# An encoder trunk's final norm begun one expert sooner, its low parts taken off GpSimd, and chunk 0 multiplied ahead of chunk 1

## The chip, the cores and the metric

The kernel runs on one core of a Trainium2 chip. The metric is device time in microseconds (us). An execution's own time holds the span of the profile, from the first to the last instruction, and about 2 us around it.

## The reference, cut to what matters

A two-layer encoder over 1024 tokens of 1024 values, in float32. Each layer is a mixer and then 16 experts; each expert takes the 128 tokens that want it most, and the results are added onto the stream. A last norm follows.

```python
def rmsnorm(x, g):
    y = x * rsqrt(mean(x * x, axis=-1) + EPS)
    return y * g

def ec_moe(h, w_router, w_gate, w_up, w_down):      # 16 experts, 128 tokens each
    aff = softmax(h @ w_router)
    gates, idx = top_k(aff.T, 128)                  # expert e: its tokens idx[e]
    xs = h[idx]
    y = silu(xs @ w_gate) * (xs @ w_up) @ w_down
    return zeros.at[idx].add(y * gates)

for i in range(2):
    x = x + mixer[i](rmsnorm(x, norm_mix[i]))       # starts with one projection h @ w_in
    x = x + ec_moe(rmsnorm(x, norm_ffn[i]), ...)
return rmsnorm(x, final_norm)
```

## The kernel before

The 1024 tokens are eight chunks of 128 rows, one row per partition. Products keep float32's accuracy by splitting each operand into a high part (`hi`, rounded by ACT's copy) and a low part (`lo = x - hi`, L232, L236, L149): `mm3` (L258) issues three matmuls for one. Weights come as pieces of 128 x 1024 values (512 KB) through the class `Stream`: `load` (L185) issues a piece's DMA on SP's queue into a free slot, `conv` (L212) makes its `hi` on ACT (L225) and its `lo` on DVE, or on POOL where `pool` is set, and gives the slot back.

**Experts** (`out_moe`, L285, called for each layer). One expert has twelve pieces: four each for the up, gate and down products. PE's order is written out by hand (L717 to 764): up of expert e with the transposes of expert e+1's rows in it (`xsT`, L581), then gate of e+1 with the transposes of e's hidden rows `sg` in it (`hT`, L624, L628), then down of e. `prod` (L620) makes `sg` on DVE after up. `index(e + 3)` (L568) makes a later expert's row numbers by eight small matmuls and gathers its rows by an indirect DMA on POOL (L578); `onehot` (L562) feeds it on DVE. `scatter` (L651) scales the result on ACT (`y`, L655) and adds it to the stream `xres` in DRAM by an indirect DMA on POOL (L659). After the products of piece j, `ahead(j)` (L593) converts up to piece j+7 into one of eight `hi`/`lo` pairs; every twelfth low part goes to POOL (`EVERY`), 15 per layer. In layer 1 the ring of slots holds 27 pieces (7 + 15 + 5). ACT, DVE and POOL each run their work in the order in which it is issued here.

**Final norm** (layer 1 alone). `final_load` (L668), after the scatter of expert 14, loads all eight chunks of `xres` on SP and gathers the rows of expert 15 as a ninth block. `final` (L694), after expert 15's down products, takes sums of squares on ACT (L690), reciprocal roots in steps (`rsqrt_steps`, L121; those of the eight chunks on POOL, with two pairs of chunks ahead of the gain row, which PE and ACT spread over the partitions, L702, L703), multiplies on DVE (`mult`, L681) and writes each chunk on SP (L685). Rows of expert 15 get its result added (L712) and are normed last and written over the chunks' rows by an indirect DMA (L715).

**Starts.** `even_proj` (L834) and `odd_proj` (L1409) begin their layer with `NormProj`: `load` a chunk, `trans` (L782) transposes it on PE and splits it (L148, L149), `stat` (L795) makes its reciprocal root on DVE, `mm` (L798) multiplies it with eight row blocks `kk` of the weights. The PSUM tiles `pt` of the transposes come from a pool of two (layer 0) or four (layer 1).

## Time and profile before

| | us |
|---|---|
| median of 3 runs (2040.78 to 2044.11) | 2043.83 |
| profiled execution, its own time | 2040.48 |
| its span | 2038.7 |
| PE busy | 1867.7 (92%) |
| DVE busy | 1507.7 (74%) |
| ACT busy | 1245.2 (61%) |
| POOL busy | 504.1 (25%) |

The experts of layer 0 lie at about 645 to 961 us, those of layer 1 at about 1690 to 2004, the final norm behind them to the end; layer 0 starts at 0, layer 1 at about 970. Shares are means over stages with different limits, so each stage is read by itself. A time in a row is in us from the span's start.

### The profile page before, as it was taken

To read this page: it belongs to the slowest core of one execution; us is meant where nothing else is said; L and a number is where in the kernel's file an instruction comes from. 1 tells how busy PE (TensorE), PEld (TensorE's weight loads), DVE (VectorE), ACT (ScalarE), POOL (GpSimd) and SP (SyncE) were. 2 spreads that over 40 slices of the span, in tenths; PEclk is the share of its full clock that TensorE was granted. 3 is DMA by queue.
4 is the path that set the end of the run, shared out by engine and by line. 5 is a ranking of instruction groups with operands and counts; after the bars stand their busy time and mean duration, and the time that the engine had idled before them with its cause. 6 is when DMAs were issued, how large, how long until landed. Compare 5 with 4: busy or idle time off the path is not lost. (4 is left out here: it accounts for less than half of the span.)

```text
span 2038.7 us, 29998 instructions
## 1 busy us (share of the span) xinstructions
PE 1867.7 (92%) x10350; PEld 1563.4 (77%) x10350; DVE 1507.7 (74%) x3092; ACT 1245.2 (61%) x2020; POOL 504.1 (25%) x426
## 2 busy tenths in 40 slices
PE   8999999998995999998998799999998968999993
PEld 6888899997883777776887688888886846777772
DVE  5431246776557999997776688889995569999994
ACT  5322257775324777776634688889883326877783
POOL 0010100002102443541002243322212014444334
PEclk9999999999997999999899999999999979999996
DMA  6232355542555999994326554424115848999955
GB/s 228 71 104 78 128 138 136 128 122 85 207 208 181 378 384 373 373 385 95 124 78 209 95 75 87 69 45 54 37 30 163 305 169 311 384 372 387 375 183 196
DMA packets 214171, 384.78 MB, mean 189 GB/s; under 512 B 71937, under 2 KB 122881, under 8 KB 214018
## 3 DMA queue, kind: packets, MB, share of 16 engines
q1 hardware_dynamic: 190082, 303.43, 45.6%
q0 software_dynamic: 21200, 73.13, 12.0%
q10 hardware_dynamic: 2736, 6.29, 0.9%
q8 instruction: 82, 1.34, 0.3%
q14 instruction: 71, 0.58, 0.1%
HBM read 309.13 MB, written 66.32 MB: 184 GB/s over the span
## 5 line engine op out<-in xcount | busy, mean ns | idle before, releaser
L232 DVE TENSOR_TENSOR lo<-raw,hi 128x1024 fp32r<-128x1024 f32 x243 | 334.0, 1416 | 12.2 <-ACT hi L225 12.2
L225 ACT ACTIVATE hi<-raw 128x1024 fp32r<-128x1024 f32 x269 | 275.1, 1055 | 15.3 <-PE py L644 12.1
L259 PE MATMUL pp<-hi,hT 128*128 128x512 f32 (+2 forms) x576 | 213.2, 370 | 0.0
L260 PE MATMUL pp<-lo,hT 128*128 128x512 f32 (+2 forms) x576 | 211.6, 367 | 0.1
L261 PE MATMUL pp<-hi,hT 128*128 128x512 f32 (+2 forms) x576 | 211.2, 367 | 0.0
L1866 DVE TENSOR_REDUCE nm<-css 128x1 f32<-128x1024 f32 x128 | 156.0, 1219 | 41.3 <-PE css L1860 40.8
L149 DVE TENSOR_TENSOR PT<-cpt,PT 128x512 fp32r<-128x512 f32 x256 | 163.1, 678 | 4.3 <-ACT PT L148 1.9
L148 ACT ACTIVATE PT<-cpt 128x512 fp32r<-128x512 f32 x256 | 139.6, 597 | 40.4 <-PE cpt L1884 38.7
L1860 PE MATMUL css<-kT,qT 128*128 128x512 f32 x512 | 151.7, 398 | 10.8 <-ACT pe L1872 9.5
L1872 ACT ACTIVATE pe<-css,nm 128x1024 f32<-128x1024 f32 x128 | 143.8, 1123 | 11.6 <-DVE rinv L1892 7.7
L1884 PE MATMUL cpt<-csident,pe 128*128 128x128 f32 x1024 | 135.0, 274 | 1.1 <-DVE PT L149 0.8
L1884 PEld LDWEIGHTS cpt<-csident,pe 128*128 128x128 f32 x1024 | 116.8, 141 | 16.3 <-DVE PT L149 3.7
L261 PEld LDWEIGHTS pp<-hi,hT 128*128 128x128 f32 x576 | 109.4, 190 | 17.5
L260 PEld LDWEIGHTS pp<-lo,hT 128*128 128x128 f32 x576 | 109.5, 190 | 17.3 <-DVE lo L236 0.3
L259 PEld LDWEIGHTS pp<-hi,hT 128*128 128x128 f32 x576 | 109.7, 190 | 17.1
L1860 PEld LDWEIGHTS css<-kT,qT 128*128 128x128 f32 x512 | 96.0, 189 | 34.6 <-ACT pe L1872 10.9
L1902 PE MATMUL po<-PT,vv 128*128 128x512 f32 x256 | 112.4, 439 | 7.1 <-DVE o L1910 7.1
L1179 DVE CUSTOM_DVE_ANT_0 sm<-ass,csnat 128x256 f32<-128x256 f32 x176 | 67.4, 420 | 52.3 <-PE ass L1177 47.6
L1903 PE MATMUL po<-PT,vv 128*128 128x512 f32 x256 | 101.6, 397 | 0.0
L232 DVE TENSOR_TENSOR cT<-raw,cT 128x1024 fp32r<-128x1024 f32 x65 | 95.7, 1492 | 3.3 <-ACT cT L225 3.2
L578 POOL DMA_INDIRECT xs<-hd,idx x32 | 65.9, 2060 | 128.3 <-DVE gt L576 128.3
L1177 PE MATMUL ass<-kT,qT 128*128 128x256 f32 x384 | 96.4, 381 | 1.0 <-DMA kT<-kT 1.0
(447 smaller groups left out, 4819.5 us busy)
## 6 DMA issues: line engine op xcount, KB each, us to landing
raw<-in_moe_w_up_dram SPq DMA_DIRECT2D x112, 512.0 KB, 6.2
raw<-in_moe_w_down_dram SPq DMA_DIRECT2D x110, 512.0 KB, 6.2
raw<-in_moe_w_gate_dram SPq DMA_DIRECT2D x106, 512.0 KB, 6.5
attn<-in_moe_w_gate_dram SPq DMA_DIRECT2D x22, 512.0 KB, 6.5
attn<-in_moe_w_down_dram SPq DMA_DIRECT2D x18, 512.0 KB, 5.9
raw<-in_even_w_in_dram SPq DMA_DIRECT2D x16, 512.0 KB, 4.7
hd<-h POOLq DMA_DIRECT2D x16, 512.0 KB, 5.5
attn<-in_moe_w_up_dram SPq DMA_DIRECT2D x16, 512.0 KB, 6.5
```

The source lines that it names most:

```text
L148: self.nc.scalar.activation(hi, src, AF.Copy)
L149: (eng or self.nc.vector).tensor_tensor(lo, src, hi.bitcast(F32), op=ALU.subtract)
L225: nc.scalar.activation(hv, tv, AF.Copy)
L232: (nc.gpsimd if pool else nc.vector).tensor_tensor(lv, tv, hv.bitcast(F32), op=ALU.subtract)
L259: nc.tensor.matmul(out, ah, bh, start=first, stop=False)
L260: nc.tensor.matmul(out, ah, bl, start=False, stop=False)
L261: nc.tensor.matmul(out, al, bh, start=False, stop=last)
L1860: nc.tensor.matmul(ss[:, n], a[:, sl], m[:, n * 512:(n + 1) * 512], start=(j == 0), stop=(j == len(passes) - 1))
L1866: nc.vector.tensor_reduce(nm, B[b]["ss"], axis=AX.X, op=ALU.max, negate=True)
L1872: nc.scalar.activation(pe, B[b]["ss"], AF.Exp, bias=B[b]["nm"], accum_out=l)
L1884: nc.tensor.transpose(pt[:, kk], B[b]["pe"][:, kc * 128:(kc + 1) * 128], k.ident)
L1902: nc.tensor.matmul(po[g], vv[:, kc], PT[g][:, 0, kc], start=(kc == 0), stop=False)
```

## The change

1. Low parts: `ahead` no longer gives any to POOL; DVE makes all.
2. Final norm: the gain row is loaded spread over the partitions by DMA. The eight chunks are loaded after the scatter of expert 13, so they lack the results of experts 14 and 15. Their squares (`fsq`) stand between the down products of expert 14 and in expert 15, their roots (`frs`, all on DVE) and multiplications there and after. After expert 14's scatter the rows of experts 14 and 15 are gathered as two blocks. Both are normed at the end and written over the chunks' rows, first those of 14, then those of 15, the latter with expert 15's result added in two halves.
3. Starts: chunk 1's transposes stand within the products of chunk 0, ahead of `kk` = 6 (layer 0) or 4 (layer 1). In layer 0 four pieces of weights are loaded ahead of chunk 1, and all four converted ahead of the first statistic.

```diff
--- before.py
+++ after.py
@@ -588,13 +588,12 @@
                 nc.tensor.transpose(pt[:, kk], d["xs"][:, c0:c0 + 128], k.ident)
             k.split(d["xh", q], d["xl", q], pt)
 
-        AHEAD, EVERY = 7, 12
+        AHEAD = 7
 
         def ahead(j):
 
             n = min(j + 1 + AHEAD, at["end"])
-            while stream.n_conv < n:
-                stream.conv(stream.n_conv + 1, pool=(stream.n_conv - at["g", 0]) % EVERY == 1, load=False)
+            stream.conv(n, load=False)
             stream.load()
 
         def gate_up(e, nm, q):
@@ -666,53 +665,54 @@
             return stream.free.pop(0)[0].tile([128, DM], F32, name="raw")
 
         def final_load():
-            f = fx["s"] = {n: wk2.tile([128, NCH + 1], F32, name=n, bufs=1) for n in ("fss", "frs")}
+            f = fx["s"] = {n: wk2.tile([128, NCH + 2], F32, name=n, bufs=1) for n in ("fss", "frs")}
+            f["s0"] = wk2.tile([128, 1], F32, name="fs0", bufs=1)
             f["g"], f["junk"] = spare(), spare()
-            f["row"] = wk2.tile([1, DM], F32, name="xs", bufs=2)
-            nc.sync.dma_start(f["row"], i["final_norm"].rearrange("(o d) -> o d", o=1))
-            f["one"] = wk2.tile([1, 128], F32, name="one", bufs=1)
-            nc.gpsimd.memset(f["one"], 1.0)
+            nc.sync.dma_start(f["g"], i["final_norm"].rearrange("(o d) -> o d", o=1).to_broadcast([128, DM]))
             for c in range(NCH):
                 fx[c] = spare()
                 nc.sync.dma_start(fx[c], xres[c * 128:(c + 1) * 128])
-            fx[NCH] = spare()
-            nc.gpsimd.indirect_dma_start(out=fx[NCH], out_offset=None, in_=xres, in_offset=rows_of(last))
+
+        def final_rows():
+            for c, e in ((NCH, last - 1), (NCH + 1, last)):
+                fx[c] = spare()
+                nc.gpsimd.indirect_dma_start(out=fx[c], out_offset=None, in_=xres, in_offset=rows_of(e))
+
+        def fsq(c, h=None):
+            f = fx["s"]
+            hs = slice(0, DM) if h is None else slice(h * 512, (h + 1) * 512)
+            nc.scalar.activation(f["junk"][:, hs], fx[c][:, hs], AF.Square, accum_out=f["s0"] if h == 0 else f["fss"][:, c:c + 1])
+
+        def frs(a, b, eps=EPS):
+            f = fx["s"]
+            for g in k.rsqrt_steps(wk2, f["frs"][:, a:b], f["fss"][:, a:b], eps, 1.0 / DM, f"fr{a}"):
+                g()
 
         def mult(c):
             f = fx["s"]
             nc.vector.scalar_tensor_tensor(fx[c], fx[c], f["frs"][:, c:c + 1], f["g"], op0=ALU.mult, op1=ALU.mult)
             if c < NCH:
                 nc.sync.dma_start(out[c * 128:(c + 1) * 128], fx[c])
-
-        def norm(a, b, on_pool):
+            else:
+                nc.gpsimd.indirect_dma_start(out=out, out_offset=rows_of(c - NCH + last - 1), in_=fx[c], in_offset=None)
+
+        def final():
+            y, gt, x = E[last]["y"], E[last]["gt"], fx[NCH + 1]
             f = fx["s"]
-            for c in range(a, b):
-                nc.scalar.activation(f["junk"], fx[c], AF.Square, accum_out=f["fss"][:, c:c + 1])
-            for g in k.rsqrt_steps(wk2, f["frs"][:, a:b], f["fss"][:, a:b], EPS, 1.0 / DM, f"fr{a}", on_pool):
-                g()
-
-        def final():
-            y, gt, x = E[last]["y"], E[last]["gt"], fx[NCH]
-            f = fx["s"]
-            for j in range(FA):
-                norm(*FG[j], j in FP)
+            frs(NCH // 2, NCH)
+            for c in range(NCH // 2, NCH):
+                mult(c)
+            fsq(NCH)
+            frs(NCH, NCH + 1)
+            mult(NCH)
             for h in range(2):
                 hs = slice(h * 512, (h + 1) * 512)
-                pt = pt2.tile([128, 512], F32, name="tp")
-                nc.tensor.matmul(pt, f["one"], f["row"][:, hs], start=True, stop=True)
-                nc.scalar.activation(f["g"][:, hs], pt, AF.Copy)
-            for j, (a, b) in enumerate(FG):
-                if j >= FA:
-                    norm(a, b, j in FP)
-                for c in range(a, b):
-                    mult(c)
-                if j == FY:
-                    for h in range(2):
-                        hs = slice(h * 512, (h + 1) * 512)
-                        nc.vector.scalar_tensor_tensor(x[:, hs], y[:, h], gt, x[:, hs], op0=ALU.mult, op1=ALU.add)
-            norm(NCH, NCH + 1, False)
-            mult(NCH)
-            nc.gpsimd.indirect_dma_start(out=out, out_offset=rows_of(last), in_=x, in_offset=None)
+                nc.vector.scalar_tensor_tensor(x[:, hs], y[:, h], gt, x[:, hs], op0=ALU.mult, op1=ALU.add)
+                fsq(NCH + 1, h)
+                if h == 0:
+                    nc.vector.tensor_scalar(f["s0"], f["s0"], 1.0 / DM, EPS, op0=ALU.mult, op1=ALU.add)
+            frs(NCH + 1, NCH + 2, f["s0"])
+            mult(NCH + 1)
 
         onehot(0)
         index(0)
@@ -740,6 +740,10 @@
                 gate_up(e, "u", q)
                 if q == 1 and more:
                     xsT(e + 1, 0)
+                if q and out is not None and not more:
+                    fsq(q + 3)
+                    if q > 1:
+                        mult(q - 2)
             prod(e)
             if more:
                 xsT(e + 1, 1)
@@ -752,16 +756,25 @@
                 act(e + 1)
             else:
                 hT(e)
+                if out is not None:
+                    fsq(7)
+                    mult(2)
+                    mult(3)
             for q in range(4):
                 down(e, q)
                 if q == 1 and e + 4 < NE:
                     onehot(e + 4)
+                if out is not None and e + 1 == last:
+                    fsq(q)
             if out is None or more:
                 scatter(e)
             else:
                 final()
+            if out is not None and e + 2 == last:
+                final_load()
             if out is not None and e + 1 == last:
-                final_load()
+                frs(0, NCH // 2)
+                final_rows()
 
 
 class NormProj:
@@ -795,12 +808,14 @@
     def stat(self, c0, c1):
         self.k.rsqrt(self.p2, self.rstd[:, c0:c1], self.ss[:, c0:c1], EPS, 1.0 / DM, f"rs{c1 - c0}")
 
-    def mm(self, c, j, n):
+    def mm(self, c, j, n, between=None):
 
         nc = self.k.nc
         pt = self.pp.tile([128, 512], F32, name="pp")
         sl = slice(c * 128, (c + 1) * 128)
         for kk in range(NCH):
+            if between and kk == between[0]:
+                between[1]()
             bh, bl = self.stream.part(j + kk // 2, kk % 2, n)
             mm3(nc, pt[:, 0:n], self.hT[:, 0, kk, sl], self.hT[:, 1, kk, sl], bh, bl, kk == 0, kk == 7)
         return pt
@@ -890,17 +905,13 @@
         def load(c):
             P.load(c, x_in[c * 128:(c + 1) * 128], nc.sync)
         load(0)
-        stream.load(2)
+        stream.load(4)
         load(1)
-        stream.load(4)
         load(2)
         load(3)
         P.trans(0)
-        stream.conv(2)
+        stream.conv(4)
         stat(0, 1)
-        stream.conv(4)
-        P.trans(1)
-        stat(1, 2)
         nc.vector.memset(von[:, :, :, 64:66], 1.0)
         j = 0
         for gi, (kind, cols) in enumerate(EVEN_GROUPS):
@@ -909,8 +920,10 @@
                 if gi + 2 == len(EVEN_GROUPS) and c == 5:
                     gx.close()
                     bg = first(ps, cv)
-                pt = P.mm(c, j, sum(n for _, n in cols))
+                pt = P.mm(c, j, sum(n for _, n in cols), (6, lambda: P.trans(1)) if gi == 0 and c == 0 else None)
                 if gi == 0:
+                    if c == 0:
+                        stat(1, 2)
                     if c + 2 < NCH:
                         P.trans(c + 2)
                         stat(c + 2, c + 3)
@@ -1465,12 +1478,12 @@
 
         P.trans(0)
         P.stat(0, 1)
-        P.trans(1)
-        P.stat(1, 2)
         for c in range(NCH):
             if c == 2:
                 k.consts(p0, "rcc", "rds", nc.gpsimd)
-            pt = P.mm(c, base, 416)
+            pt = P.mm(c, base, 416, None if c else (4, lambda: P.trans(1)))
+            if c == 0:
+                P.stat(1, 2)
             if c + 2 < NCH:
                 P.trans(c + 2)
                 P.stat(c + 2, c + 3)
```

## Rows read from the trace of the kernel before

**Rows 1.** Busy time by stretch: expert 7, expert 13, plain loads.

```profile
core 0: us, PE busy (x) PEld busy (x) DVE busy (x) ACT busy (x) POOL busy (x), PEclk, DMA share, GB/s
1836.30:1855.70 19.40, 18.51 (x94) 14.79 (x93) 18.98 (x19) 15.13 (x18) 9.07 (x3) 1.00 1.02 378
1954.45:1972.60 18.15, 18.15 (x85) 14.64 (x84) 16.70 (x17) 15.14 (x18) 4.00 (x2) 1.00 0.41 125
2005.00:2006.00 1.00, 1.00 (x3) 0.18 (x1) 0.00 (x0) 0.00 (x0) 0.77 (x4) 1.00 1.04 430
```

**Rows 2.** POOL in order of time: start, duration, line, operation [idle before, releaser].

```profile
1721.94 4.86 POOL L659 DMA_INDIRECT xb<-y,idx  x1 [7.77 <-PE pu L261]
...
1843.17 3.00 POOL L232 TENSOR_TENSOR cT<-raw,cT 128x1024 fp32r<-128x1024 f32 x1
...
1955.84 1.60 POOL L659 DMA_INDIRECT xb<-y,idx  x1 [7.74 <-ACT y L655]
```

**Rows 3.** DVE in order of time, layer 1, in two experts.

```profile
1834.21 2.35 DVE L232 TENSOR_TENSOR lo<-raw,hi 128x1024 fp32r<-128x1024 f32 x2
...
1843.27 4.00 DVE L232 TENSOR_TENSOR cT<-raw,cT 128x1024 fp32r<-128x1024 f32 x1 [0.42 <-ACT cT L225]
```

**Rows 4.** PE in order of time, the same expert.

```profile
1847.92 0.66 PE L628 MATMUL tp<-csident,sg 128*128 128x128 f32 x4 [0.89 <-DVE sg L622]
```

**Rows 5.** Who PE waited for, 1740 to 2000, then 1690 to 1745: total, times, longest.

```profile
PE tp L628 <- DVE sg L622: 10.5, 12, 0.9
...
PE tp L628 <- DVE sg L622: 2.7, 2, 1.7
```

**Rows 6.** What SP's queue waited for, 1650 to 2000.

```profile
SPq L202 <- DVE lo L232: 68.1, 60, 4.3
```

**Rows 7.** PE in order of time, start of layer 0.

```profile
11.79 1.94 PE L790 MATMUL pt<-csident,xin 128*128 128x128 f32 x8 [4.84 <-DMA xin<-in_x_dram]
```

**Rows 8.** PE in order of time, start of layer 1.

```profile
971.78 2.12 PE L790 MATMUL pt<-csident,xin 128*128 128x128 f32 x8 [10.74 <-DMA xin<-xa]
...
977.04 0.69 PE L259 MATMUL pp<-hi,hT 128*128 128x416 f32 x1
```

**Rows 9.** ACT in order of time, experts 14 and 15 and the final norm.

```profile
1985.13 0.60 ACT L618 ACTIVATE sg<-pg 128x512 f32<-128x512 f32 x1 [0.31 <-PE pg L261]
...
1990.71 1.12 ACT L655 ACTIVATE y<-py,gt 128x1024 f32<-128x1024 f32 x1 [0.28 <-PE py L644]
...
2011.46 1.06 ACT L690 ACTIVATE raw<-raw 128x1024 f32<-128x1024 f32 x1
2012.42 0.19 ACT L690 ACTIVATION_READ_ACCUMULATOR raw<-raw 128x1 f32 x1
```

**Rows 10.** DVE in order of time, expert 15 and the final norm.

```profile
1996.31 0.69 DVE L622 TENSOR_TENSOR sg<-pu,sg 128x512 f32<-128x512 f32 x1 [2.28 <-PE pu L261]
...
2010.85 2.48 DVE L683 SCALAR_TENSOR_TENSOR raw<-raw,frs 128x1024 f32<-128x1024 f32 x2 [11.78 <-POOL fr_t L136]
...
2030.09 0.15 DVE L130 TENSOR_SCALAR fr_xe<-fss 128x1 f32<-128x1 f32 x1
...
2032.26 1.28 DVE L683 SCALAR_TENSOR_TENSOR raw<-raw,frs 128x1024 f32<-128x1024 f32 x1
```

**Rows 11.** PE in order of time, down products of expert 15.

```profile
1998.40 0.74 PE L644 MATMUL py<-hi,th 128*128 128x512 f32 x2 [0.69 <-ACT th L148]
...
2003.85 0.40 PE L644 MATMUL py<-hi,tl 128*128 128x512 f32 x1
```

**Rows 12.** POOL in order of time, final norm.

```profile
1992.10 1.55 POOL L659 DMA_INDIRECT xb<-y,idx  x1 [12.20 <-ACT y L655]
...
1998.95 1.01 POOL L679 DMA_INDIRECT raw<-xb,idx  x1 [5.25 <-issue]
...
2033.88 1.06 POOL L715 DMA_INDIRECT out_dram<-raw,idx  x1 [6.22 <-DVE raw L683]
```

**Rows 13.** SP's queue in order of time, final norm.

```profile
1998.23 3.95 SPq L677 DMA_DIRECT2D raw<-xb  x8
```

## The prediction

> **What bounds the kernel now.** The run spends most of its time in long stages; the change touches four places, so I read each of them by itself. First the table of busy time by stretch over the experts of layer 1 [rows 1]: in one expert's 19.4 us VectorE (DVE) is busy 18.98 us, TensorE (PE) 18.51, ACT 15.13, POOL 9.07, and the DMA engines all the time. In the expert after that (1954.45 to 1972.60) PE is busy for the whole of its 18.15 us. So PE alone needs 18.15 us for an expert, and something adds 1.3 us in the others. Next the order of time on POOL [rows 2]: the scatters of experts 0 and 12 start at 1721.94 and 1955.84, twelve experts in 233.90 us, 19.49 us each. (Layer 0 looks the same.) Then who waits for whom [rows 4, 5]: PE waits 0.89 us per expert, twelve times, at the transposes of the hidden rows (L628) for DVE's product `sg` (L622). Last what DVE does before that product [rows 2, 3]: POOL starts its low part at 1843.17 for 3.00 us; DVE starts one of its own at 1843.27 and takes 4.00 us for it, where two in a row take 2.35. It ends 1.0 us after POOL's does: it did nothing until POOL was through, then ran its usual time. Both layers hold 30 such low parts on POOL, and DVE has exactly 30 low parts that are that long, one beside each: 26 of 3.8 to 4.1 us and four of 2.65 (the last two experts of each layer, where POOL begins earlier and PE waits for nothing).
>
> The end is another stage: PE's last product of an expert starts at 2003.85 [rows 11], the span ends at 2038.7, and the final norm fills what lies between. The two starts are bounded by PE waiting for chunk 1 of the rows [rows 7, 8].
>
> **Low parts from POOL to DVE.** Removed: 15 POOL low parts per layer, and with each a block of DVE of 4.00 − 1.21 = 2.8 us. Added: one more DVE low part per expert, 2.35 − 1.21 = 1.14 us in a row of them. DVE needs 18.98 − 2.8 + 1.14 = 17.3 us per expert, less than PE. In the stretch before L628 DVE now has two low parts one behind the other: from 1843.27, or a little before, 2.3 us instead of 4.0, the product at 1845.6 instead of 1847.2. PE got there at 1847.03 and waited until 1847.92 [rows 4]. So the wait goes, with 0.7 us to spare behind the product's 0.69, and PE is late next. Its period is then the 18.15 us of the expert without a wait and the eight index matmuls which that one lacks; with them PE is busy 18.51 us [rows 1], so it lies between the two. I take 18.41, nearer to the second. Gain: 12 experts × (19.49 − 18.41 = 1.08) = 13 us per layer; in expert 0 PE waits 1.7 us at L628 [rows 5], of which the block gives back 1.5. Two layers: 2 × 14.5 = **29.0 us**. Bounds: 2 × 12 × (19.49 − 18.15) + 3.4 = 35 if the index costs nothing; below, 22, if a quarter of the wait comes back elsewhere, since DVE still is 94% busy. Work on POOL itself costs nothing: its gathers and scatters only get an emptier queue.
>
> **Does DMA allow it?** One expert moves 378 GB/s × 19.4 us = 7.33 MB; in 18.4 us that is 398 GB/s. The chip gives 430 in one later stretch of plain loads [rows 1]. Even if weights could not come faster than 378, they are ahead: SP waits 68 us for slots that DVE has to release [rows 6], so the ring of 27 pieces is full; and the weights are all there in the stretch from 1954 (share 0.41), while ACT still converts in the last expert but one. Losing 1.08 us per expert to DMA uses up 14 us of a lead of some 30.
> The Trainium skill's page "SBUF — State Buffer" (section "A bandwidth-pool intuition that's wrong") speaks against the change: HBM, about 358 GB/s to a core, is almost always the end-to-end bound. By it an expert would take 7.33 MB / 358 = 20.5 us, and no engine change would help; the rows' 378 and 430 GB/s are already above that figure, so it gets a small chance only, as a rival below.
>
> **Start of layer 0.** Now PE transposes chunk 0, waits 4.84 us for chunk 1, transposes it, and only then multiplies chunk 0 [rows 7]. After, 18 of the 24 products may run in that wait, and at best all of it comes back. But they need converted weights, pieces 2 and 3 are loaded ahead of chunk 1, so that chunk 1 lands two pieces (some 2.6 us at the 400 GB/s of the rows) later, and DVE has four pieces' low parts and a statistic queued before chunk 1's low parts, whose PSUM buffers chunk 2's transposes need. Rather under half of the 4.84: **2.2 us** (1 to 3.5).
>
> **Start of layer 1.** Transposes of chunk 0 end at 973.9 (971.78 + 2.12), products begin at 977.04 [rows 8]; chunk 1's landing and transposes lie between. After, twelve products start in that gap and chunk 1's transposes follow them. At best 3.1 us come back, nothing if chunk 1's statistic and low parts, now behind, hold up chunk 1's products by as much. I take half, **1.6 us** (0 to 3).
>
> **The final norm.** Loads of the rows move from behind the scatter of expert 14 to behind that of expert 13, 18.15 us earlier, and lie beside products with the DMA engines idle. The path, on before's clock:
> ACT in expert 14's down products: now `sg` at 1985.13, four conversions, `y` at 1990.71 [rows 9]. After, four squares of 1.06 + 0.19 us lie between them: 0.5 + 4 × 1.0 + 4 × 1.25 puts `y` at 1994.7, 4 us late. Queued behind: the scatter (1.39 us after `y`'s start [rows 9, 12]), so at 1996.1, and the two row gathers 6.85 us after it (1992.10 to 1998.95 [rows 12]), at 2003; if they land as a scatter does, 6.1 us later (1992.10 to SP's 1998.23 [rows 13]), their squares are done by 2010.3.
> DVE: reciprocal roots of chunks 0 to 3 after the fourth square, 1994.7 to 1996.9 (2030.09 to 2032.26 is 2.17 us [rows 10]); the last low part to 1998.1; two multiplications (2.48 [rows 10], 2.4 in a row) to 2000.5; only then the product `sg`, which ran at 1996.31. So PE idles over 4 us, and its down products begin 2.1 us behind that (1996.31 to 1998.40 [rows 10, 11]), at 2002.6, and end 5.8 later (1998.40 to 2004.2 [rows 11]). This costs nothing at the end because DVE is later: `tl` 2003.2, two multiplications 2005.6, roots 2007.8, four multiplications 2012.6, roots 2014.8, multiplication 2016.1 for expert 14's rows. Then the last rows: two additions (0.7 each, like the product of that size [rows 10]) with two half squares between and behind (0.8 each) and one small step, 2019.2; roots 2021.4; multiplication 2022.7; scatter at 2023.0, and the same 4.8 us to the end (2033.88 to 2038.7): 2027.9. Gain **10.8 us**. Were PE's clock to halve in its idle time, the down products take 11.6 us and end at 2014.2, still 2 us before DVE needs them. The write of expert 14's rows starts at 2016.4 and has 6.6 us before the next must follow; a scatter took 6.1. Bounds: 6 (both row writes at 7 us or more, one more wait of ACT) to 15 (ACT not full). The two broadcast products and copies of the gain row, and POOL's roots, vanish; the gain row's broadcast load has nothing to wait for.
>
> **Sum.** 29.0 + 2.2 + 1.6 + 10.8 = 43.6 us. The profiled execution: 2040.48 us (span 2038.7 and 1.8 around it), so 1996.9. The median of the runs, 2043.83, lies 3.3 above it; from there 2000.2. I say **1999 us**.
>
> **Rivals.** (1) *The end brings little*: ACT's and DVE's new work ahead of `sg`, or the row writes in series, eat it; 6 us or less instead of 10.8 and the starts at their low ends: 2005 to 2012. For: ACT full, one DVE queue. Chance 0.14. (2) *DMA is the bound of the experts*: the period stays at 19.4 because the lead is smaller than it looks; only the end, the starts and the first experts gain, 15 to 18 us: 2026. Against: SP's waits for slots. Chance 0.07. That POOL's low parts were not what PE waited for gives the same time. (3) *DVE becomes the bound*, slower: if its long operation has a cause of its own, DVE needs 18.98 + 1.14 us and its 0.4 us of idle time, 20.5 per expert, 24 experts × 1.05 = 25 us lost against 14.6 gained: 2054. It decides from where over 2.4 of the 2.8 us of block remain (17.3 + 2.4 + 0.4 = 20.1, 0.6 over the period, 24 × 0.6 = 14.6). Against: thirty blocks beside thirty low parts, each ending 1 us after POOL's. Chance 0.04.
>
> **Numbers.** Forecast 0.75, rivals 0.14, 0.07 and 0.04. Range: the lower bounds together, 22 + 6 + 1 + 0 = 29, from the median give 2015; the experts at their upper bound and the rest as forecast, 35 + 14.6 = 50, from the profiled execution give 1990 (all upper bounds at once, 56, I leave out). So 1990 to 2014, which takes in most of rival 1; rivals 2 and 3 stay outside. Faster by over 0.2% (what a measurement here can tell from no change): 0.94; within: 0.02; slower: 0.04.
>
> **What would show it.** No DVE low part above 1.3 us in the experts; scatter to scatter 18.4 us; no wait of PE at L628; DMA share still near 1. In the last expert, PE idle over 4 us before L628 and DVE without a gap from 1994 to the last scatter. Scatters 19.4 us apart would make it wrong by 26 us; a last scatter later than 30 us behind expert 14's `y` would break the sum of the end.

## The result and the profile after

| | before | after |
|---|---|---|
| median | 2042.99 us (2040.78 to 2044.11) | 1997.86 us (1995.87 to 1999.71) |
| ratio | | 0.978, 95% interval 0.9763 to 0.9797 |
| profiled execution: own time, span | 2040.48, 2038.7 us | 1999.71, 1997.9 us |
| DVE busy, one expert of layer 1 | 18.98 of 19.40 us [rows 1] | 17.61 of 18.40 us |
| PE's waits for the product `sg` | 26.8 us, 28 times | 5.2 us, 4 times (3.9 of it in the last expert) |

The kernel is 45 us faster; the prediction said 1999 us. The two profiled executions are 40.8 us apart, because that of before was a short one of its kernel and that of after a long one. The scatters of the experts cut this difference into stretches, and beside each stands what the prediction had put there:

| stretch | before | after | gain | predicted |
|---|---|---|---|---|
| start to scatter 0, layer 0 | 678.98 | 674.68 | 4.3 | 2.2 + 1.5 = 3.7 |
| scatter 0 to 15, layer 0 | 283.63 | 269.93 | 13.7 | 13.0 |
| on to scatter 0, layer 1 | 759.33 | 761.47 | -2.1 | 1.6 + 1.5 = 3.1 |
| scatter 0 to 13, layer 1 | 252.05 | 238.63 | 13.4 | 13.0 |
| scatter 13 to the end | 64.71 | 53.17 | 11.5 | 10.8 |

Only the third stretch is off, by 5 us; e8, e11 and e12 show that this stretch varies about as much between executions of one and the same kernel.

After, busy time by stretch, from scatter to scatter: an expert in the middle of layer 1, and the expert in which the loads run out (columns as in [rows 1]):

```profile
1834.68:1853.08 18.40, 18.40 (x93) 14.98 (x92) 17.61 (x20) 15.25 (x18) 3.60 (x2) 1.00 1.03 388
1926.61:1944.71 18.10, 18.10 (x85) 14.71 (x85) 16.38 (x16) 15.13 (x18) 1.59 (x1) 1.00 0.77 282
```

PE is busy for the whole of the 18.40 us: it is the bound now (the weights' DMA lies near, see e10). DVE has 0.8 us to spare, and the DMA engines have work in the second row for 0.77 of the time, where it was 0.41 before [rows 1]: the weights run less far ahead.

After, POOL in order of time, the scatters of experts 0, 6, 7 and 12 of layer 1; 0 and 12 answer to [rows 2]:

```profile
1706.08 4.83 POOL L658 DMA_INDIRECT xb<-y,idx  x1 [6.67 <-ACT y L654]
...
1834.68 1.82 POOL L658 DMA_INDIRECT xb<-y,idx  x1 [9.06 <-ACT y L654]
1853.08 1.82 POOL L658 DMA_INDIRECT xb<-y,idx  x1 [9.08 <-ACT y L654]
...
1926.61 1.59 POOL L658 DMA_INDIRECT xb<-y,idx  x1 [9.07 <-ACT y L654]
```

Scatter 0 to scatter 12 is 220.53 us, 18.38 us per expert (18.34 in layer 0), where it was 19.49.

After, DVE in order of time, in front of the product; it answers to [rows 3]:

```profile
1838.27 2.35 DVE L232 TENSOR_TENSOR lo<-raw,hi 128x1024 fp32r<-128x1024 f32 x2
1840.54 0.68 DVE L621 TENSOR_TENSOR sg<-pu,sg 128x512 f32<-128x512 f32 x1
```

Two low parts in 2.35 us stand where one took 4.00. No low part of DVE in the experts is longer than 1.23 us.

PE in order of time, at the two starts: before, the third chunk's transposes in layer 0 and the second chunk's first product in layer 1:

```profile
20.82 1.03 PE L790 MATMUL pt<-csident,xin 128*128 128x128 f32 x8
...
983.69 0.44 PE L259 MATMUL pp<-hi,hT 128*128 128x416 f32 x1
```

After, answering to [rows 7] and [rows 8]:

```profile
9.41 0.80 PE L259 MATMUL pp<-hi,hT 128*128 128x512 f32 x1 [2.33 <-ACT hi L235]
...
18.36 1.25 PE L803 MATMUL pt<-csident,xin 128*128 128x128 f32 x8
...
953.72 2.23 PE L803 MATMUL pt<-csident,xin 128*128 128x128 f32 x8 [10.69 <-DMA xin<-xa]
...
955.65 0.71 PE L259 MATMUL pp<-hi,hT 128*128 128x416 f32 x1
...
963.53 0.43 PE L259 MATMUL pp<-hi,hT 128*128 128x416 f32 x1
```

In layer 0 the third chunk's transposes start at 18.36, where they started at 20.82: 2.5 us. In layer 1 products begin 1.9 us behind the start of the first transposes; before it was 5.3 (971.78 to 977.04).

### The profile page after: what moved, and what is told of

The parts are those of the page before. It is cut to its first block, busy times and chain, and to the rows that moved or that the text cites. A ratio compares the mean times of both kernels' runs of the same rounds, so it can differ in the third digit from the quotient of the medians.

```text
span 1997.9 us, 29943 instructions
## 1 busy us (share of the span) xinstructions
PE 1864.8 (93%) x10346; PEld 1568.7 (79%) x10346; DVE 1473.5 (74%) x3160; ACT 1244.9 (62%) x2022; POOL 352.4 (18%) x337
## 5 line engine op out<-in xcount | busy, mean ns | idle before, releaser
L232 DVE TENSOR_TENSOR lo<-raw,hi 128x1024 fp32r<-128x1024 f32 x260 | 310.1, 1227 | 24.2 <-ACT hi L225 23.0
L225 ACT ACTIVATE hi<-raw 128x1024 fp32r<-128x1024 f32 x269 | 275.2, 1055 | 14.5 <-PE py L643 10.2
L1879 DVE TENSOR_REDUCE nm<-css 128x1 f32<-128x1024 f32 x128 | 156.0, 1218 | 41.5 <-PE css L1873 40.8
L1873 PEld LDWEIGHTS css<-kT,qT 128*128 128x128 f32 x512 | 96.0, 189 | 34.6 <-ACT pe L1885 10.8
L578 POOL DMA_INDIRECT xs<-hd,idx x32 | 70.2, 2195 | 197.5 <-DVE gt L576 197.5
L259 PE MATMUL pp<-hi,aTh 128*128 128x512 f32 x208 | 87.3, 420 | 0.4 <-DVE o L1226 0.4
```

What stands on the lines that cost most here:

```text
L225: nc.scalar.activation(hv, tv, AF.Copy)
L232: (nc.gpsimd if pool else nc.vector).tensor_tensor(lv, tv, hv.bitcast(F32), op=ALU.subtract)
L259: nc.tensor.matmul(out, ah, bh, start=first, stop=False)
L1873: nc.tensor.matmul(ss[:, n], a[:, sl], m[:, n * 512:(n + 1) * 512], start=(j == 0), stop=(j == len(passes) - 1))
L1879: nc.vector.tensor_reduce(nm, B[b]["ss"], axis=AX.X, op=ALU.max, negate=True)
```

## The experiments

The three parts of the change alone, each put into the kernel before.

**e1: no low parts on POOL.**

```diff
-                stream.conv(stream.n_conv + 1, pool=(stream.n_conv - at["g", 0]) % EVERY == 1, load=False)
+            stream.conv(n, load=False)
```

> The kernel before with one part of the change alone: no low part of an expert's weights is taken by POOL, DVE takes all of them. Start and final norm stay as before. Theory (a low part on POOL stops DVE's low part beside it for 2.8 us, and that is what PE waits for): the period of scatters of layer 1, experts 0 to 12, falls from 19.49 to 18.4 us, no low part of DVE in the experts is longer than 1.4 us, PE's waits for the product sg fall from 26.8 us to under 8, and the kernel is 29 us faster (22 to 35): ratio 0.986. Rival A (the weights' DMA or something else sets the period): period 19.4, ratio 1.000. Rival B (DVE's long operation has a cause of its own, so that DVE only gets more to do): period over 20 us, ratio 1.012.

Measured: ratio 0.9855 (0.9839 to 0.9872), 30 us; period 18.38 us in layer 1 and 18.32 in layer 0. This part alone gives what it was to give, and rivals A and B are out.

**e2: the final norm.**

```diff
+            if out is not None and e + 2 == last:
+                final_load()
...
+                frs(0, NCH // 2)
+                final_rows()
```

> The kernel before with the final norm of the change alone: loads behind the scatter of expert 13, norm over the rows as they are without the last two experts, and those two experts' rows written over. Experts and starts as before. Theory: from the down products of expert 14 on it gains 11 us (prediction 10.8; between sg of expert 15 and the end the two profiles differ by 11.5), ratio 0.9946. Rival A (the gain of the end is small, and the difference of 45 us between the two kernels is mostly from the experts): 6 us or less, ratio 0.997 or more. Rival B (the end gains more alone, because without the new experts DVE is nowhere ahead): more than 13 us, ratio under 0.9935.

Measured: ratio 0.9940 (0.9924 to 0.9957), 12 us. From the scatter of expert 13 to the end it takes 53.18 us, the changed kernel 53.17, the kernel before 64.71: the end gains the same with the old experts ahead of it. The interval of the times (9 to 15 us) would leave room for rival B; the 11.5 us of the traces don't.

**e3: the two starts.**

```diff
-        P.trans(1)
-        stat(1, 2)
...
-                pt = P.mm(c, j, sum(n for _, n in cols))
+                pt = P.mm(c, j, sum(n for _, n in cols), (6, lambda: P.trans(1)) if gi == 0 and c == 0 else None)
```

> The kernel before with the two starts of the change alone: chunk 0 multiplied ahead of chunk 1's transposes in both layers. Theory: chunk 2's transposes come 2.4 us earlier in layer 0 and chunk 1's products 2.1 us earlier in layer 1, as in the changed kernel; nothing behind them takes it back, so the kernel is 4 us faster (3 to 5), ratio 0.998. Rival (what follows, weights or the queues of DVE and ACT, is late by itself and takes the lead back): under 1.5 us, ratio 0.9993 to 1.0005. In the changed kernel 4 to 5 us of the lead went lost at the end of layer 1's attention, where PE waits 8.9 us at po for o in place of 2.5; if the starts cause that, it is seen here too.

Measured: ratio 0.9981 (0.9970 to 0.9991), 3.9 us, with room from 1.8 to 6.1. PE's wait at `po` is 4.91 us here, neither of the two values of the expectation; e11 and e12 take it up. The three ratios multiplied give 0.9777; the whole change has 0.978. As far as the intervals tell (some 0.0015 to either side), the parts neither help nor hinder each other.

**What a low part on POOL costs.** e1 shows the gain, not that its price is the 2.8 us of the prediction.

**e4: two on POOL instead of one.**

```diff
-        AHEAD, EVERY = 7, 12
+        AHEAD, EVERY = 7, 6
```

> The kernel before with POOL taking two of an expert's twelve low parts instead of one (every sixth instead of every twelfth). Theory (each low part on POOL costs DVE 2.8 us and saves it 1.14): DVE needs 17.3 + 2 x 1.66 = 20.6 us per expert, and with its 0.4 us of idle time the period is 21.0 us; 24 experts x 1.5 = 36 us slower, and some 4 more in the experts 0 and those at the end, ratio 1.018 to 1.020; there are 60 low parts of DVE of 3.8 to 4.1 us. Rival (the offload takes work off DVE, and PE's wait for sg is only a matter of where the one low part lies): period 19.5 or less, ratio 0.995 to 1.000.

Measured: ratio 0.9958 (0.9943 to 0.9972), and a period of 18.86 us, not 21.0. The expectation was wrong in sign: two on POOL are faster than one, and the 60 long low parts of DVE take 2.6 to 3.4 us, not 3.8 to 4.1. So the price is no constant. The next rows show it, first those of before, in the expert of [rows 3]; [rows 2] has a scatter as long (4.86 us), of which the prediction made nothing. POOL and then DVE in order of time:

```profile
1838.90 4.82 POOL L659 DMA_INDIRECT xb<-y,idx  x1 [7.75 <-ACT y L655]
```

```profile
1836.48 1.22 DVE L565 TENSOR_TENSOR oh<-csslots,slot 128x1024 bf16<-128x1024 f32 x1
1837.62 3.49 DVE L232 TENSOR_TENSOR lo<-raw,hi 128x1024 fp32r<-128x1024 f32 x3
1841.03 1.22 DVE L232 TENSOR_TENSOR cT<-raw,cT 128x1024 fp32r<-128x1024 f32 x1
1842.16 0.68 DVE L149 TENSOR_TENSOR xl<-tp,xh 128x512 fp32r<-128x512 f32 x1
```

A scatter that meets nothing takes 1.55 us (expert 14's, [rows 12]). This one takes 4.82, and it ends 1.55 us after 1842.16, the moment when DVE comes to the end of an unbroken row of operations on two SBUF inputs and starts one that reads PSUM (`xl`). The same holds for all 24 long scatters of before (1.53 to 1.59 us). So POOL is held up as well. The piece of its low part, queued behind the scatter, is converted on ACT by 1842.29, and where the scatter is short the low part follows that conversion by 0.14 us; here it begins at 1843.17, 0.7 us late, and the scatter's record even goes on to 1843.72 (records on POOL are rough). By then DVE has only its next low part to do, and that one is kept out for the whole length of POOL's.

With two on POOL, POOL and then DVE in order of time, in layer 1:

```profile
1832.01 2.51 POOL L659 DMA_INDIRECT xb<-y,idx  x1 [2.32 <-ACT y L655]
1835.53 3.18 POOL L232 TENSOR_TENSOR cT<-raw,cT 128x1024 fp32r<-128x1024 f32 x1 [1.01 <-ACT cT L225]
...
1845.62 2.99 POOL L232 TENSOR_TENSOR lo<-raw,hi 128x1024 fp32r<-128x1024 f32 x1 [2.42 <-ACT hi L225]
```

```profile
1835.24 1.21 DVE L232 TENSOR_TENSOR cT<-raw,cT 128x1024 fp32r<-128x1024 f32 x1
1836.37 0.68 DVE L149 TENSOR_TENSOR xl<-tp,xh 128x512 fp32r<-128x512 f32 x1
1836.97 2.82 DVE L232 TENSOR_TENSOR cT<-raw,cT 128x1024 fp32r<-128x1024 f32 x1
...
1846.48 3.20 DVE L232 TENSOR_TENSOR cT<-raw,cT 128x1024 fp32r<-128x1024 f32 x1
```

Here the scatter gets through at about 1832.97 (its end less 1.55), between two low parts, and POOL's first low part begins on time. It waits until DVE's operation is through (1836.37) and then runs 2.34 us, 0.6 of them beside `xl`, which isn't held up. DVE loses 2.82 - 1.21 = 1.6 us to it, and 3.20 - 1.21 = 2.0 to the second, where before it lost 2.8. By this DVE needs 17.6 - 2 x 1.14 + 3.6 = 18.9 us, and the measured period is 18.86.

**e5: one on POOL, in another place.**

```diff
-                stream.conv(stream.n_conv + 1, pool=(stream.n_conv - at["g", 0]) % EVERY == 1, load=False)
+                stream.conv(stream.n_conv + 1, pool=(stream.n_conv - at["g", 0]) % EVERY == 7, load=False)
```

> The kernel before with the one low part on POOL taken half an expert later (the eighth of the twelve in place of the second). Theory as the runs so far leave it: POOL's tensor operation and DVE's operations on two SBUF inputs shut each other out; in the place of before POOL's low part stands right behind its scatter, which DVE's unbroken row of low parts holds up until 1842.16, so it begins late, at the moment when DVE has nothing but the next low part to do, and DVE loses 2.8 us; in the other place, as the run with two on POOL shows, it begins during a DVE operation and costs DVE 2.0 us for 1.14 saved. DVE then needs 17.61 - 1.14 + 2.0 = 18.5 us per expert, PE 18.4: period 18.4 to 18.7, the kernel 20 to 27 us faster than before, ratio 0.987 to 0.990. Rival (one low part on POOL costs the same wherever it stands, 2.8 us, as the prediction had it): period 19.3 to 19.5, ratio 0.998 to 1.000.

Measured: ratio 0.9878 (0.9855 to 0.9902), period 18.39 us. One low part on POOL costs 1.1 us per expert in one place and nothing in the other. POOL and then DVE in order of time:

```profile
1832.29 2.75 POOL L232 TENSOR_TENSOR lo<-raw,hi 128x1024 fp32r<-128x1024 f32 x1 [1.53 <-ACT hi L225]
```

```profile
1833.15 2.97 DVE L232 TENSOR_TENSOR cT<-raw,cT 128x1024 fp32r<-128x1024 f32 x1 [0.38 <-ACT cT L225]
```

DVE's low part still ends 1.08 us after POOL's, so it was kept out here too; but it loses 1.8 us, and with 17.6 - 1.14 + 1.8 = 18.2 us DVE stays under PE's 18.4. The loss grows from expert to expert, in this run from 1.4 to 2.0 us, at which DVE comes level with PE.

**e6 and e7: an extra operation on POOL**, added to the changed kernel in layer 0 alone; in e7 the last line is a copy, `nc.gpsimd.tensor_copy(scr, hi)`.

```diff
+                if layer == 0 and (m - at["g", 0]) % 12 == 1:
+                    hi = stream.pair[m][0].bitcast(F32)
+                    scr = wk2.tile([128, 1024], BF16, name="scr", bufs=1)
+                    nc.gpsimd.tensor_tensor(scr, hi, hi, op=ALU.subtract)
```

> The changed kernel with an extra operation on POOL in layer 0's experts alone: where POOL had its low part before, it subtracts the same converted piece from itself into a scratch tile that nothing reads (two SBUF inputs, 128x1024); DVE keeps all low parts. Layer 1 is the control within the run. Theory (POOL's tensor operation shuts DVE's out): DVE needs 17.6 + 1.7 to 2.8 = 19.3 to 20.4 us, period of layer 0 from scatter 0 to scatter 12 is 19.3 to 20.6 us against 18.34 without it, layer 1 stays at 18.38; 12 to 26 us slower than the changed kernel, ratio to before 0.984 to 0.991. Rival (DVE's long low parts of before have a cause of their own): 18.34 in both layers, no low part of DVE over 1.3 us, ratio 0.978.

> The same with a copy in place of the subtraction: POOL's extra operation in layer 0 reads one SBUF tile and writes one (128x1024). Theory A (any tensor operation of POOL on SBUF shuts out DVE's operations on two SBUF inputs): DVE operations beside it end about 1.1 us after POOL's, period of layer 0 over 18.8 us. Theory B (only an operation with two SBUF inputs does): no DVE low part over 1.4 us, period of layer 0 18.34 us, time as the changed kernel's, ratio 0.978.

Measured in e6: scatter 0 to 12 of layer 0 at 20.00 us per expert, layer 1 at 18.38; ratio 0.989 (0.9867 to 0.9914). DVE's operations are the same as in the changed kernel, so POOL's operation alone does it. POOL, then DVE, in order of time, in e6:

```profile
783.27 2.48 POOL L602 TENSOR_TENSOR scr<-hi 128x1024 bf16<-128x1024 f32 x1
```

```profile
782.87 5.11 DVE L232 TENSOR_TENSOR lo<-raw,hi 128x1024 fp32r<-128x1024 f32 x2
```

Two low parts of 2.35 us take 5.11. In e7 the copy is shorter, and so is the loss:

```profile
777.64 1.63 POOL L602 CAST scr<-hi 128x1024 bf16<-128x1024 f32 x1
```

```profile
777.28 4.22 DVE L232 TENSOR_TENSOR lo<-raw,hi 128x1024 fp32r<-128x1024 f32 x2
```

4.22 - 2.35 = 1.9 us for a copy of 1.63; period of layer 0 19.24 us, ratio 0.9819 (0.9795 to 0.9842). Theory A of e7: one SBUF input on POOL's side is enough (the copy writes SBUF too; the runs don't tell the two apart).

**e8 and e9: the end in another order**, beside the changed kernel itself (e8, no edit).

```diff
+            fsq(NCH)
+            frs(NCH // 2, NCH + 1)
+            for c in range(NCH // 2, NCH + 1):
+                mult(c)
...
+                frs(0, NCH // 2)
                 hT(e)
...
+                    for c in range(NCH // 2):
+                        fsq(c + 4)
+                        mult(c)
...
+                final_rows()
+                for c in range(NCH // 2):
+                    fsq(c)
```

> The changed kernel itself once more, as the yardstick for the next run: 1996 to 2000 us, ratio to before 0.978.

> The changed kernel with the end in another order: the squares of chunks 0 to 3 stand behind expert 14's y in place of between the conversions ahead of it; the reciprocal roots of chunks 0 to 3 and the multiplications of chunks 0 and 1 stand behind expert 15's product sg in place of ahead of it; the squares of chunks 4 to 7 behind expert 15's hidden rows; one row of reciprocal roots for chunks 4 to 7 and expert 14's rows together; and the small step on the half sum of squares behind both additions. Theory (from expert 14's y on DVE sets the end, as the prediction has it): one set of roots less is 2.1 us, the small step no longer keeps the second addition waiting 0.8 us, expert 14's y is 2.9 us earlier; the distance from the scatter of expert 13 to the end falls from 53.2 to 50 us (49.5 to 52), PE no longer waits 3.9 us for sg; time 1.5 to 4 us below the changed kernel's of this set, ratio to before 0.9765. Rival (PE's wait for sg or ACT's squares set the end as much as DVE does, and the squares now come behind everything): distance 53 or more, no gain or up to 2 us slower.

Measured: the changed kernel 1994.73 us, ratio 0.9779 (0.9762 to 0.9795); the other order 1994.78 us, 0.9789 (0.9774 to 0.9805). (e8's median lies 1.3 us below the 1996 to 2000 expected, its ratio is as expected.) From the scatter of expert 13 to the end e9 takes 53.52 us against 53.60: nothing. Part of the savings isn't there: `y` of expert 14 comes 2.9 us sooner, but its scatter only 1.4 (19.56 us behind that of expert 13, 20.92 in e8), and PE still waits 3.0 us for `sg`. DVE and then POOL at the end of e9:

```profile
1973.96 6.07 DVE L693 SCALAR_TENSOR_TENSOR raw<-raw,frs 128x1024 f32<-128x1024 f32 x5
...
1984.33 1.28 DVE L693 SCALAR_TENSOR_TENSOR raw<-raw,frs 128x1024 f32<-128x1024 f32 x1
```

```profile
1983.48 0.99 POOL L697 DMA_INDIRECT out_dram<-raw,idx  x1 [15.87 <-DVE fr_t L136]
1987.58 0.98 POOL L697 DMA_INDIRECT out_dram<-raw,idx  x1 [3.12 <-DMA out_dram<-raw,idx]
```

The last multiplication ends at 1985.61, 46.7 us behind the scatter of expert 13 (47.6 in e8, 48.1 in the first profile of the changed kernel, below). But the last write isn't issued before 1987.58: it waits for the write of expert 14's rows, and that one, whose rows were ready at 1980.0, was issued only at 1983.48, 4.7 us after the last chunk's multiplication (1973.96 + 4 x 1.20 = 1978.8). The row names DVE's `fr_t`, which this write doesn't need; the last wait of POOL's queue ahead of it was for the landing of a chunk's write, until 1982.35. Neither DVE nor PE sets the end here, but three writes to the same rows, one after the other. So the rival's numbers hold but not its cause, and this is no version that beats the changed kernel.

**e10: how near the weights' DMA is.**

```diff
-            stream.conv(n, load=False)
+            stream.conv(n, load=False, low=False)
...
+                nc.tensor.matmul(d[nm], d["xh", h][:, kk - 4 * h], hi[:, w], start=kk == 0, stop=False)
+                nc.tensor.matmul(d[nm], d["xl", h][:, kk - 4 * h], hi[:, w], start=False, stop=kk == 7)
```

> The changed kernel without the low parts of the experts' weights (but for the first four pieces of a layer): DVE makes none, PE leaves out the third of the products that reads them, so that the result is coarser. DMA and ACT have the same work. PE needs 18.4 x 2/3 = 12.3 us per expert, DVE 17.6 - 12 x 1.14 = 3.9, ACT is busy for 15.25. This shows how far the weights' DMA is from being the bound. Theory (the DMA engines, busy all the time at 388 GB/s, still have room): an expert's bytes, 388 GB/s x 18.38 us = 7.13 MB, come at the 430 GB/s of a later stretch in 16.6 us, period 16.4 to 17.2, 40 to 60 us faster. Rival (388 GB/s is all there is, and the changed kernel lives on the weights loaded ahead): period 18.0 to 18.4 us once those are used up.

Measured: 1946.32 us in its one run, 48 under e8 and so within the theory's 40 to 60, but not by its period. The first five periods of a layer are 14.3 to 14.5 us; then the weights loaded ahead are used up, the engines wait for data, and six experts of layer 1 take (busy time by stretch):

```profile
1751.91:1865.86 113.95, 90.84 (x400) 71.44 (x400) 22.86 (x41) 90.70 (x103) 15.46 (x12) 0.85 1.03 390
```

That is 18.99 us per expert at 390 GB/s, 7.4 MB. The theory's 430 GB/s is not to be had in this mix, and the rival's 18.0 to 18.4 us is too low as well: the DMA floor lies above the period of the changed kernel, which lives on the weights loaded ahead. How many those are, e10 shows too: its twelve periods take 204.8 us, 23 less than 12 x 18.99. SP's queue shows it: what it waited for in the changed kernel, 1700 to 1950 (total, times, longest):

```profile
SPq L202 <- DMA raw<-in_moe_w_gate_dram: 40.5, 28, 3.1
SPq L202 <- DMA raw<-in_moe_w_down_dram: 34.1, 30, 2.1
SPq L202 <- DVE lo L232: 30.1, 30, 2.1
```

In the same stretch of before the wait of L202 for DVE's `lo` was 61.6 us (68.1 in the longer one of [rows 6]), and none for a load was among its costliest. Now SP waits for its earlier loads to land, as it does nearly all the time in e10.

**e11 and e12: the missing 5 us.** In the third stretch of the table the changed kernel lost 2.1 us instead of gaining. PE in order of time, end of layer 1's attention, in the changed kernel:

```profile
1527.08 0.80 PE L1915 MATMUL po<-PT,vv 128*128 128x512 f32 x1 [8.93 <-DVE o L1923]
```

Just ahead of it ACT, which DVE's `o` waits for, is kept by a load:

```profile
1523.88 0.63 ACT L148 ACTIVATE aTh<-aT 128x512 fp32r<-128x512 f32 x1 [8.21 <-DMA aT<-oda]
```

The same wait of PE was 2.48 us in the profile of before (1538.27 [2.48 <-DVE o L1910]; ACT waited 0.27 there), and up to there the engines' orders of instructions are the same in the kernel before and in e2's, which waits 9.02. Nothing is edited; each kernel ran once more.

> The kernel before once more, for one look at the end of layer 1's attention, where PE waited 2.5 us at po for o in its profile and 8.9 us in that of the changed kernel, though both issue the same instructions in the same order there. If the wait goes with the kernel as it was built, it is 2.5 us (2 to 3) again; if it goes with the single execution, it may be anything from 1.5 to 9.5.

> The kernel with the final norm of the change alone once more, for the same look: its wait was 9.0 us. With the kernel as built: 8.5 to 9.5 us again; with the single execution: anything from 1.5 to 9.5. From the scatter of expert 13 to the end it took 53.2 us in its first profile, and should again (52.5 to 54).

Measured: the wait of before, run again, and that of e2's kernel, run again:

```profile
1542.20 0.80 PE L1902 MATMUL po<-PT,vv 128*128 128x512 f32 x1 [9.53 <-DVE o L1910]
```

```profile
1535.37 0.50 PE L1916 MATMUL po<-PT,vv 128*128 128x512 f32 x1 [1.46 <-DVE o L1924]
```

The two have changed places: 2.48 and 9.53 us with one kernel, 9.02 and 1.46 with the other. It belongs to the single execution, not to a kernel. Through all the profiles it lies between 1.46 and 9.55 us. In four of the five long ones (after, e2, e9, e11) ACT waits 8.2 to 8.8 us for `aT<-oda`; in e8 it is another transfer (`odb<-o`). Why they land late was not followed further.

The wait is not the whole of the 5 us. Between its two profiles the kernel before differs by 7.05 us in the wait and by 2.9 in the stretch, e2's kernel by 7.6 and 3.1, and the changed kernel itself by 0.7 and 4.7 (after and e8). In before and after PE is idle for the same time in this stretch (65.6 and 65.5 us); it is busy 2.2 us longer in after, 696.0 against 693.7, with the same number of instructions. What the difference is made of stays open.

The whole third stretch is 759.3, 762.2, 759.9 and 756.8 us in before, e11, e2 and e12, which have the old starts and experts, and 761.5, 753.6, 753.2, 756.8 and 756.0 in after and e6 to e9, which have the new ones: 759.6 and 756.2 in the mean. That is a gain of 3.4 us where 3.1 were predicted and the two single profiles gave -2.1; with so wide a spread in so few profiles it agrees with the prediction but doesn't show it. From the scatter of expert 13 to the end, e2's kernel took 53.22 us the second time, and the kernel before 64.22.

## Why the prediction was right, step by step

- *Low parts, 29.0 us.* 30 us in e1 (26 to 33 by the interval). The period was to be 18.41 and is 18.38 and 18.34; PE's wait is gone and PE is late next, as said. DVE was to need 17.3 us and is busy 17.61. (The expert of 18.15 us from which the prediction took PE's need is expert 13, not the one after expert 7; and two of its sums are a little off, 35.6 us for the upper bound of 35, 1.03 for rival 3's 1.05. Neither moves the forecast.)
- *The price of the block.* Right for the place where the low part stood (2.8 us, e6: 5.11 - 2.35 = 2.76), wrong as a general price: 1.6 and 2.0 us in e4, 1.4 to 2.0 in e5. The prediction read the long low parts of DVE but not the long scatter ahead of POOL's, 4.6 to 4.9 us in 12 rows of each layer. "Work on POOL itself costs nothing" missed the other direction too: DVE's row keeps POOL out, and so POOL's low part comes late enough to cost its whole length. That the lateness does it is argued from these rows and from e4 and e5, where the low part is on time; no run changes it alone. The forecast didn't hang on it: the change takes all low parts off POOL.
The Trainium skill has the rule on its page "SBUF — State Buffer", section "SBUF: two separate sides": VectorE and GpSimd share a pair of ports as an exclusive lock; an operation of VectorE on two SBUF inputs and one of GpSimd that reads SBUF keep each other out for the whole instruction. The rows agree for the tensor operations (DVE's ends 1.0 to 1.1 us after POOL's in before, e4 and e5), and for `xl`, which reads PSUM and runs its 0.68 us beside POOL. They differ for the scatter, which was kept out for more than one instruction: past two boundaries in DVE's row of before, to its end.
- *Does DMA allow it?* The answer was right, one of its two reasons was not. 430 GB/s, read from a stage of plain loads, is out of reach here: 388 in the changed kernel, 390 in e10. What held was the lead, 23 us by e10 where the prediction said some 30 without a source. At 18.38 against 18.99 us per expert the change uses up 0.6 us x 12 = 7 us of it per layer, not the 14 of the prediction (which took before's 19.4 us for the floor). A second change of that size in the experts (period 17.3) would use 20 of the 23, an estimate from these numbers, and leave next to nothing for a third.
The Trainium skill's rule on its page "SBUF — State Buffer", section "A bandwidth-pool intuition that's wrong", that HBM with about 358 GB/s is almost always the bound, would have 7.4 MB take 20.7 us, an estimate from that figure; e10 has 18.99 us. As a rule it is nearly true of this stage; as a figure it is lower than what this kernel drew.
- *Starts, 2.2 and 1.6 us.* 2.5 us in layer 0 by the third chunk's transposes. In layer 1 the second chunk's products start 9.8 us behind the first transposes (963.53 and 953.72), where it was 11.9 (983.69 and 971.78): 2.1 us. Together 3.9 us in e3 against 3.8, though its interval reaches from 1.8 to 6.1.
- *Final norm, 10.8 us.* 11.5 us in the stretch, 12 in e2. The steps, counted from the scatter of expert 13 (1973.99 and 1944.71):

| step | predicted | measured |
|---|---|---|
| `y` of expert 14 | 20.7 (4 us late) | 19.6 (2.8 late) |
| gather of its rows issued | 29.0 | 27.9 |
| product `sg` of expert 15 | 26.5 | 25.5 |
| down products begin | 28.6 | 28.0 |
| multiplications of chunks 4 to 7 | 33.8 to 38.6 | 33.2 to 38.1 |
| last multiplication ends | 48.7 | 48.1 |
| last write issued | 49.0 | 48.4 |
| end | 53.9 | 53.2 |

ACT fitted the four squares in with 1.2 us less delay than reckoned, and 0.5 to 1.1 us of it run through the chain. The changed kernel's end, DVE, then POOL, in order of time:

```profile
1970.19 0.68 DVE L621 TENSOR_TENSOR sg<-pu,sg 128x512 f32<-128x512 f32 x1
1972.71 0.69 DVE L149 TENSOR_TENSOR tl<-tp,th 128x512 fp32r<-128x512 f32 x1 [1.84 <-ACT th L148]
1973.32 2.47 DVE L693 SCALAR_TENSOR_TENSOR raw<-raw,frs 128x1024 f32<-128x1024 f32 x2
1977.95 4.87 DVE L693 SCALAR_TENSOR_TENSOR raw<-raw,frs 128x1024 f32<-128x1024 f32 x4
1984.92 1.28 DVE L693 SCALAR_TENSOR_TENSOR raw<-raw,frs 128x1024 f32<-128x1024 f32 x1
...
1987.70 0.15 DVE L713 TENSOR_SCALAR fs<-fs 128x1 f32<-128x1 f32 x1 [0.84 <-ACT raw L684]
...
1991.49 1.28 DVE L693 SCALAR_TENSOR_TENSOR raw<-raw,frs 128x1024 f32<-128x1024 f32 x1
```

```profile
1965.65 1.55 POOL L658 DMA_INDIRECT xb<-y,idx  x1 [19.37 <-ACT y L654]
1972.58 1.00 POOL L679 DMA_INDIRECT raw<-xb,idx  x1 [5.38 <-DMA xb<-y,idx]
...
1988.32 0.99 POOL L697 DMA_INDIRECT out_dram<-raw,idx  x1 [12.88 <-issue]
1993.06 0.98 POOL L697 DMA_INDIRECT out_dram<-raw,idx  x1 [3.75 <-DVE raw L693]
```

Two things were not as said. DVE isn't without a gap, as the signs had it: it waits 1.84 us for the hidden rows and 0.84 us at L713, a small step that waits for ACT's half square and keeps the second addition waiting. The sum itself had room for these waits, and so its total holds. And the write of expert 14's rows was to start as soon as they were multiplied; it started 2.1 us after that (1986.2 to 1988.32), because the chunks' own writes to the same rows must have landed. The prediction gave that write 6.6 us of room, and 4.7 were left. They just sufficed in this execution; in e8 and e9 the last write had to wait for it.
- *PE's idle time before expert 15's transposes*, over 4 us predicted, is 3.93 us and costs nothing, as said. What the prediction allowed for did happen: after it the granted clock is 0.50 (1.2 GHz) in the first 2.7 us of the down products and 1.00 in their last 1.6, and they take 7.5 us where they took 5.85 at 1.00 before. They are done at 1980.2, and DVE came to expert 15's additions at 1986.12.

## What to carry to other kernels

Where one engine's operation takes a multiple of its usual time, look at what the other one does in that moment, and at what made that one late: an operation offloaded to POOL can cost DVE its whole length and a little more (1.9 us for 1.63, 2.8 for 2.48) while DVE works on two SBUF inputs, and the place in the order decides whether that is anybody's wait (1.1 us per expert in one place, nothing in another). For whether the DMA has room, a rate must be taken from the same mix of transfers. A row that is written over by a later one puts the landings of both writes into the chain at the end.

## What the runs showed of the hardware

- A scatter with indices issued by POOL takes 1.55 us when nothing meets it and 4.82 beside an unbroken row of DVE operations on two SBUF inputs; it then ends 1.53 to 1.59 us after the row does. In most experts of e4 and e5 it got in at the first boundary inside a row (1.7 to 2.5 us). Why one boundary lets it in and another doesn't stays open.
- A copy on POOL with one SBUF input keeps DVE out as well: 1.9 us for a copy of 1.63 us.
- One wait of PE in the attention, behind rows that go through DRAM, varied from 1.46 to 9.02 us and from 2.48 to 9.53 between two executions of the same program; the stretch around it varied by 2.9 to 4.7 us. That is more than the start of a layer is worth, and a single profile can't tell the two apart.
- After 3.93 us without work for PE the granted clock was 0.50 in the next products and rose to 1.00 within them; the 24 products took 7.5 us in place of 5.85.
